# A two-layer hybrid diffusion step on one core: where the three branch output projections keep their operands, and what they wait for

## The chip, the cores and the metric

One core of a Trainium2 chip runs the whole program. The metric is the time of one execution in device microseconds (us); lower is better. TensorE (PE in the profile) multiplies, VectorE (DVE), ScalarE (ACT) and GpSimd (POOL) work element by element, SyncE (SP) issues all transfers, in the order in which they are written.

## The reference, cut to what matters

Each of two layers takes 1152 tokens (1024 latent, 128 context) of width 1024:

```
h = RMSNorm(x) * (1 + scale) + shift
P = h @ W_in                      # queries, keys, values, z paths, merge gates of all mixers
oa, ob, oc = attention, retention, gated DeltaNet (4 heads of 128 each)
y_b = (rms_norm(o_b) * silu(z_b)) @ W_branch[b]            # b = 0, 1, 2: 512 -> 1024
x = x + gate * ((sum_b sigmoid(G_b) * y_b) @ W_out)
```

In the kernel all tokens stand in the free dimension: h is held as 8 blocks of 128 features by 1152 tokens, every head's output o as 128 by 1152.

## The kernel before, in words

**Precision.** A product in full precision is made of three products of a rounded type: an operand is split into a high part (a cast on ScalarE) and a low part (the rest, a subtraction), and high x high, high x low and low x high are added in PSUM. The normalised input is kept so in two fixed tiles, `hH` and `hL` (8 blocks each). Weights are loaded, cast (L648, ACT) and subtracted (L652, POOL) by `load_w`.

**Streams.** A layer is cut into streams (generators): projections for retention (`rp`), DeltaNet (`fk`, `fq`, `fv`), attention values (`av`) and queries and keys (`prep0` to `prep3`), 12 z paths (`z`), 24 merge gates (`g`), for layer 0 also the next layer's conditioning (`ada`). All of these read `hH` and `hL` (matmuls of L677 and L698). Then there are chains that go from engine to engine: retention (`rm`), DeltaNet (`mid`, `pp`, `scan`), and attention, `mix0` to `mix3`, one for each head, one after another behind the last DeltaNet scan. Each chain ends in `put_o`, which transposes the head's output (L1014), multiplies by the z path (L1016) and stores it in DRAM (`osc`, L1017).

**Branches.** `branch` multiplies four heads by `W_branch`. In the order in which they run, the first is that of retention (`br1`), the second that of DeltaNet (`br2`), the third that of attention (in `fin`, ahead of the product with `W_out`, L1936). Each loads the four heads from `osc` (L1854), casts them (L1855, ACT), subtracts (L1856, DVE) and then makes 24 tiles of 128 features by 384 tokens: 12 matmuls (L1879), a multiplication by the gate (L1882, DVE; the gate's tile comes from DRAM, `ssc`), and from the second branch on an addition (L1884, DVE) of the sum so far, which comes from DRAM too (`ysc`). The first two store the sum to `ysc`; the third writes it, split, into `hH` and `hL`. Before the change the split heads take 8 of 25 pages of SBUF.

**What sets the order.** An emitter picks, again and again, the ready stream that stands first: chains first, then the list `BULK`; a stream may start when those it depends on (third argument of `add`) are done and enough pages are free (`NEED`). Then a list scheduler (`Order`) with a priority for each instruction (`LEAD`, `EVAC` shift it) fixes the order on every engine. The engines keep that order on the chip.

Of the kernel before, what the change touches and what calls it, by code (L numbers as in the profile page):

```python
# [33 lines left out]
LAG = 2  # L34
SGN = 3
QO = 'sync'
NP = ()
EVAC = 32000
SC, BK, PV = (2, 3, 4), (5, 6), 7
SLOW, LATE, SLOWD = 0.93, 0, 1.265  # L40
CHAIN = ('pp', 'scan', 'rm', 'mid', 'mix')
BULK = "rp0 z10 fv0 rp1 fk3 fk0 z11 fq1 z13 fk1 fq0 fv1 z12 fq2 g17 z22 z23 fv2 av0 fv3 z20 g13 prep0 g12 g04 g22 g14 fk2 prep3 av1 prep1 g27 z21 z00 g23 g20 gate0 g21 g10 g11 g26 z01 g00 fq3 g15 z02 g03 g16 g01 g25 g02 g07 prep2 br2 z03 g06 g05 ada fin br1 g24".split()
NEED = {'rp': 10, 'rm': 6, 'fk': 6, 'mid': 4, 'fq': 5, 'fv': 6, 'pp': 2, 'scan': 1, 'av': 10, 'prep': 9, 'mix': 5, 'z': 3, 'g': 3, 'gate': 6, 'ada': 6, 'fin': 16, 'br': 14}
LEAD = {'mix': 4000, 'scan': 0, 'mid': 500, 'pp': 0, 'rm': 0, 'fv': 200, 'prep': 4000, 'fq': 0, 'fa': 1000}

K_CS, K_TRI, K_REL, K_ONE, K_LIN, K_ID, K_BLK, K_MH, K_SEL, K_I32, K_END = (
    0, 1024, 1280, 1536, 1664, 1668, 1796, 1800, 1836, 1838, 1870)
# [506 lines left out]
class Build:  # L554
# [181 lines left out]
    def layer(self, l):  # L736
# [1099 lines left out]
    def branch(self, l, br, bi):  # L1836


        nc, ar, ap = self.nc, self.ar, self.ap
        last = bi == 2  # L1840
        self.store(0)
        seq = [ap["w_branch"][l, br, :, fp * 256:fp * 256 + 256] for fp in range(4)]
        held = []

        def weights():

            while seq and len(held) < (FD if held else 1):
                held.append(self.load_w([seq.pop(0)], 4))
            return held.pop(0)

        hl = []
        for h in range(NH):
            o, hb, lb = ar.alloc(T), ar.alloc(T, True), ar.alloc(T, True)
            nc.sync.dma_start(out=o.v(T), in_=self.osc[l][br][h])  # L1854
            nc.scalar.copy(hb.v(T), o.v(T))  # L1855
            nc.vector.tensor_tensor(out=lb.v(T), in0=o.v(T), in1=hb.v(T).bitcast(F32), op=ALU.subtract)  # L1856
            o.free()
            hl.append((hb, lb))
        tr = Ring(ar, 384, 3)
        pr = Ring(ar, 384, 3) if bi else None  # L1860
        yield 0, 8, 5
        for fp in range(4):
            w, wh, wl = weights()
            for fi in range(2):
                f = 2 * fp + fi
                for tb in range(3):
                    c = slice(tb * 384, tb * 384 + 384)
                    t = tr.next().v(384)
                    nc.sync.dma_start(out=t, in_=self.ssc[l][br][f][:, c])
                    y = t  # L1870
                    if bi:
                        y = pr.next().v(384)
                        nc.sync.dma_start(out=y, in_=self.ysc[l][f][:, c])
                    out = self.ps[:, self.bank(1, (0, 1, 2, 3)) if last else self.bulk(), 0:384]
                    i = 0
                    for hb, lb in hl:
                        h = i // 3
                        for ww, a in ((wh, hb), (wh, lb), (wl, hb)):
                            nc.tensor.matmul(out=out, lhsT=ww[:, h, fi * 128:fi * 128 + 128], rhs=a.v(T)[:, c], start=i == 0, stop=i == 11)  # L1879
                            i += 1  # L1880
                    with self.lead(EVAC):
                        nc.vector.scalar_tensor_tensor(out=t, in0=t, scalar=1.0, in1=out, op0=ALU.add, op1=ALU.mult)  # L1882
                    if bi:
# [147 lines left out]
```

## Time and profile before

| | |
|---|---|
| median of 3 runs (lowest, highest) | 3273.01 us (3272.86 to 3279.33) |
| profiled execution | 3282.82 us |
| its span, first to last instruction | 3281.0 us |
| TensorE busy | 3124.0 us, 95% |
| mean granted clock of TensorE | 0.979 of full speed |

The profiled execution is 9.8 us longer than the median of the timed runs; 1.8 us of its time lie outside the span. The busy share of TensorE counts a matmul from issue to its modelled end, so it says when TensorE had nothing to do, not how near it is to its peak.

### The profile page before, as it was taken

How to read it: one execution, taken by the hardware profiler on the slowest of the kernel's cores; microseconds unless marked ns; L12 is line 12 of the kernel's file. 1: busy time of each engine (PE TensorE's matmuls, PEld its weight loads, DVE VectorE, ACT ScalarE, POOL GpSimd, SP SyncE). 2: the span in 40 equal slices, each digit the busy share in tenths (PEclk: the TensorE clock that was granted, in tenths of full speed). 3: DMA queues.
4: the chain of work that ended last, by engine and by line, in shares of the span. 5: the costliest groups of instructions: out<-in, count | busy, mean ns of one | idle time of the engine just before them, and what ended most of it. 6: DMA issues, size and time to landing. Idle time of an engine off the chain costs nothing.

```text
span 3281.0 us, 59199 instructions
## 1 busy us (share of the span) xinstructions
PE 3124.0 (95%) x22411; PEld 2957.9 (90%) x22411; DVE 1887.3 (58%) x4625; ACT 1358.1 (41%) x3982; POOL 1009.9 (31%) x1366
## 2 busy tenths in 40 slices
PE   7999999999999998979999999999999999979799
PEld 6999999999999987878799998999999989969787
DVE  5536566665355558655455365656654657676452
ACT  5324455354354546522233244544443535554120
POOL 3222244343442213113132214443335143221140
PEclk9999999999999999989999999999999999989999
DMA  6122324423121161278322223233232121124771
GB/s 217 57 84 89 93 72 132 121 64 100 51 64 59 42 204 50 93 237 261 120 84 73 83 79 99 81 97 96 68 94 60 42 69 35 54 71 148 243 254 52
DMA packets 328401, 335.73 MB, mean 102 GB/s; under 512 B 58165, under 2 KB 293043, under 8 KB 328115
## 3 DMA queue, kind: packets, MB, share of 16 engines
q1 hardware_dynamic: 328114, 331.95, 32.3%
q8 instruction: 176, 2.88, 0.4%
q14 instruction: 111, 0.90, 0.1%
HBM read 239.43 MB, written 92.44 MB: 101 GB/s over the span
## 4 chain that ended last, share of the span: by engine, by line
PE 81%; DMA 8%; DVE 5%; ACT 3%; issue 2%; POOL 1%; SPq 0%; DVEq 0%; ACTq 0%; POOLq 0%
PE ps L698 34%; PE ps L677 14%; PE ps L1936 6%; PE ps L1879 5%; PE ps L1772 4%; PE ps L1803 4%; PE ps L1794 2%; DMA pg<-ssc 2%; DMA pg<-in_w_in 1%; PE ps L1582 1%; DMA pg<-in_w_ada 1%; DMA pg<-ysc 1%; PE ps L1577 1%; PE ps L1590 1%; PE ps L1574 1%
## 5 line engine op out<-in xcount | busy, mean ns | idle before, releaser
L698 PE MATMUL ps<-hH,pg 128*128 128x384 f32 x4608 | 1274.2, 346 | 11.1 <-ACT pg L648 5.6
L652 POOL TENSOR_TENSOR pg<-pg,pg 128x256 fp32r<-128x256 f32 (+1 forms) x704 | 549.2, 809 | 1212.7 <-ACT pg L648 777.4
L698 PEld LDWEIGHTS ps<-hH,pg 128*128 128x128 f32 x4608 | 835.8, 189 | 19.9 <-ACT pg L648 6.5
L698 PE MATMUL ps<-hL,pg 128*128 128x384 f32 x2304 | 789.7, 343 | 0.0
L677 PE MATMUL ps<-pg,hH 128*128 128x256 f32 (+1 forms) x2880 | 545.6, 287 | 9.0 <-DVE pg L1683 3.8
L677 PEld LDWEIGHTS ps<-pg,hH 128*128 128x128 f32 x2880 | 449.4, 189 | 16.6 <-DVE pg L1683 6.0
L698 PEld LDWEIGHTS ps<-hL,pg 128*128 128x128 f32 x2304 | 435.0, 189 | 1.6
L677 PE MATMUL ps<-pg,hL 128*128 128x256 f32 (+1 forms) x1440 | 407.6, 284 | 0.6 <-DVE hL L942 0.6
L1879 PE MATMUL ps<-pg,pg 128*128 128x384 f32 x1728 | 336.4, 347 | 53.4 <-ACT pg L648 38.8
L1879 PEld LDWEIGHTS ps<-pg,pg 128*128 128x128 f32 x1728 | 309.3, 193 | 60.2 <-ACT pg L648 40.5
L677 PEld LDWEIGHTS ps<-pg,hL 128*128 128x128 f32 x1440 | 271.5, 189 | 2.1 <-DVE hL L942 0.8
L648 ACT CAST pg<-pg 128x1024 fp32r<-128x1024 f32 (+1 forms) x176 | 184.0, 1049 | 183.6 <-DMA pg<-in_w_in 76.3
L627 POOL TENSOR_TENSOR lo<-lo,kc 128x12 f32<-128x12 f32 (+4 forms) x94 | 143.8, 1530 | 363.4 <-DVE lo L1694 88.1
L1335 DVE SCALAR_TENSOR_TENSOR pg<-pg,lo,pg 128x384 f32<-128x384 f32 (+2 forms) x288 | 191.7, 669 | 72.1 <-ACT pg L1333 67.6
L1772 PE MATMUL ps<-pg,pm 128*128 128x384 f32 x768 | 214.3, 371 | 6.7 <-ACT pg L1776 6.4
L1776 ACT ACTIVATE pg<-ps,lo 128x384 f32<-128x384 f32 (+1 forms) x300 | 168.7, 572 | 82.9 <-DVE lo L1774 81.7
L1773 DVE TENSOR_REDUCE lo<-ps 128x1 f32<-128x384 f32 (+1 forms) x300 | 158.9, 543 | 74.2 <-PE ps L1772 72.4
L1936 PE MATMUL ps<-pg,hH 128*128 128x512 f32 x576 | 185.4, 402 | 5.0 <-POOL pg L652 3.8
L968 ACT ACTIVATE pg<-ps 128x384 f32<-128x384 f32 x144 | 70.6, 490 | 199.0 <-PE ps L698 196.8
L1772 PEld LDWEIGHTS ps<-pg,pm 128*128 128x128 f32 x768 | 130.0, 197 | 21.3 <-ACT pg L1776 14.1
L1803 PE MATMUL ps<-pg,pg 128*128 128x128 f32 x1040 | 141.0, 283 | 8.1 <-ACT pg L1799 4.7
L1803 PEld LDWEIGHTS ps<-pg,pg 128*128 128x128 f32 x1040 | 132.9, 197 | 12.2 <-ACT pg L1799 7.0
(300 smaller groups left out, 4908.1 us busy)
## 6 DMA issues: line engine op xcount, KB each, us to landing
pg<-in_w_in SPq DMA_DIRECT2D x112, 512.0 KB
ssc<-pg SPq DMA_DIRECT2D x144, 192.0 KB
pg<-ssc SPq DMA_DIRECT2D x144, 192.0 KB
pg<-in_w_ada SPq DMA_DIRECT2D x48, 512.0 KB
pg<-gsc SPq DMA_DIRECT2D x32, 576.0 KB
ysc<-pg SPq DMA_DIRECT2D x96, 192.0 KB
pg<-ysc SPq DMA_DIRECT2D x96, 192.0 KB
zsc<-pg SPq DMA_DIRECT2D x72, 192.0 KB
```

The source lines that it names most:

```text
L627: self.nc.gpsimd.tensor_tensor(out=out, in0=in_, in1=self.mh[0:in_.shape[0], 0:in_.shape[1]], op=ALU.pow)
L648: nc.scalar.copy(h, r)
L652: (nc.vector if dve else nc.gpsimd).tensor_tensor(out=lo[:, c], in0=r[:, c], in1=h[:, c].bitcast(F32), op=ALU.subtract)
L677: nc.tensor.matmul(out=out, lhsT=a[:, k, t * 128:t * 128 + 128], rhs=x[:, k % 4, :], start=i == 0, stop=i == 23)
L698: nc.tensor.matmul(out=out, lhsT=w[:, k, :], rhs=a[:, k, tb * 384:tb * 384 + 384], start=i == 0, stop=i == 23)
L1335: nc.vector.scalar_tensor_tensor(out=o, in0=x[:, lo + s:hi + s], scalar=wcol(s), in1=o, op0=ALU.mult, op1=ALU.add)
L1772: nc.tensor.matmul(out=self.ps[:, b, 0:w], lhsT=q[:, i, m], rhs=k, start=i == 0, stop=i == 1)
L1773: nc.vector.tensor_reduce(out=s[:, m * 3 + c:m * 3 + c + 1], in_=self.ps[:, b, 0:w], op=ALU.max, axis=AX.X)
L1776: nc.scalar.activation(out=p.v(T)[:, c * w:c * w + w], in_=self.ps[:, bs[c], 0:w], func=AF.Exp, bias=s[:, 6 + m:7 + m], accum_out=s[:, 8 + ...
L1803: nc.tensor.matmul(out=oo, lhsT=x[:, i * 128:i * 128 + 128], rhs=v, start=kt == 0, stop=kt == nkt - 1)
L1879: nc.tensor.matmul(out=out, lhsT=ww[:, h, fi * 128:fi * 128 + 128], rhs=a.v(T)[:, c], start=i == 0, stop=i == 11)
L1936: nc.tensor.matmul(out=out, lhsT=a, rhs=ww[:, f % 2, :], start=j == 0, stop=j == 23)
```

## The change

The split heads of the first two branches go into `hH` and `hL` (blocks 0 to 3 and 4 to 7), which hold the normalised input until the last projection has read them. So `br1` now depends on every gate, every z path, `av1`, `prep3` and `scan3`; `br2` on `br1` alone. `fin` depends on `mix2` and no longer on `mix3`; its branch loads three heads, and waits for `mix3` (the `yield` ahead of the fourth) before it emits the load of the fourth. `NEED` of branches falls from 14 to 8, of `fin` from 16 to 14. The loads, casts and subtractions of heads get a lead of 600. `EVAC`, three entries of `LEAD` and the list `BULK` are replaced. No matmul is added or removed.

```diff
+HL = 600
-EVAC = 32000
+EVAC = 16000
-BULK = "rp0 z10 fv0 rp1 fk3 fk0 ... g06 g05 ada fin br1 g24".split()
+BULK = "rp1 z10 rp0 fk3 fk0 fv0 ... z03 br1 ada g03 g06 g07".split()
-NEED = {..., 'fin': 16, 'br': 14}
+NEED = {..., 'fin': 14, 'br': 8}
-LEAD = {'mix': 4000, ..., 'prep': 4000, 'fq': 0, 'fa': 1000}
+LEAD = {'mix': 8000, ..., 'prep': 0, 'fq': 8000, 'fa': 4000}
...
-        add("br1", self.branch(l, 1, 0), ["rm1"] + [f"g1{f}" for f in range(8)])
-        add("br2", self.branch(l, 2, 1), ["br1", "scan3"] + [f"g2{f}" for f in range(8)])
-        add("fin", self.finish(l), ["br2", "mix3"] + gs + zs + ["gate0"] * (l == 0) + ["ada"] * (not last))
+        add("br1", self.branch(l, 1, 0), ["rm1", "scan3", "av1", "prep3"] + gs + zs)
+        add("br2", self.branch(l, 2, 1), ["br1"])
+        add("fin", self.finish(l), ["br2", "mix2"] + ["gate0"] * (l == 0) + ["ada"] * (not last))
...
-        hl = []
+        hl, own = [], []
         for h in range(NH):
-            o, hb, lb = ar.alloc(T), ar.alloc(T, True), ar.alloc(T, True)
-            nc.sync.dma_start(out=o.v(T), in_=self.osc[l][br][h])
-            nc.scalar.copy(hb.v(T), o.v(T))
-            nc.vector.tensor_tensor(out=lb.v(T), in0=o.v(T), in1=hb.v(T).bitcast(F32), op=ALU.subtract)
-            o.free()
+            if last and h == NH - 1:
+                yield (f"mix{h}.{l}",)
+            with self.lead(HL):
+                o = ar.alloc(T)
+                if last:
+                    own.append((ar.alloc(T, True), ar.alloc(T, True)))
+                    hb, lb = (x.v(T) for x in own[-1])
+                else:
+                    hb, lb = self.hH[:, 4 * bi + h, :], self.hL[:, 4 * bi + h, :]
+                nc.sync.dma_start(out=o.v(T), in_=self.osc[l][br][h])
+                nc.scalar.copy(hb, o.v(T))
+                nc.vector.tensor_tensor(out=lb, in0=o.v(T), in1=hb.bitcast(F32), op=ALU.subtract)
+                o.free()
             hl.append((hb, lb))
```

Lines ahead of `branch` are one higher in the changed kernel (L678 for L677, L1773 for L1772, L1015 for L1014), those in it ten higher (L1889 for L1879, L1892 for L1882, L1894 for L1884).

**First place: TensorE in layer 0, from the end of the projections.** Before, 143 rows of attention and of its transposes stand between the last projection and the first matmul of a branch; these are the last of them (L1794, L1803: `mix2`; L1014: its `put_o`; from L1752 on `mix3`).

```order
L1794 MATMUL ps<-kc,pg_692_10849 128x128
L1803 MATMUL ps<-pm_3_391,pg_672_10737 128x128
L1014 MATMUL ps<-kc,pg_510_7648 128x128 x9
L1752 MATMUL ps<-kc,pm_10_941 128x128 x4
L1772 MATMUL ps<-pm_143_13013,pm_152_13196 128x128 x4
L1772 MATMUL ps<-pg_812_13011,pm_103_9388 128x384 x2
L1752 MATMUL ps<-kc,pm_10_941 128x128 x2
L1772 MATMUL ps<-pg_812_13011,pm_103_9388 128x384 x4
L1752 MATMUL ps<-kc,pm_10_941 128x128 x2
L1794 MATMUL ps<-kc,pg_189_2692 128x128
L1879 MATMUL ps<-pg_801_12388,pg_848_13276 128x384
```

Now the first matmul of the first branch (L1889, on `hH`) stands 18 rows behind the last projection (L678), in the midst of `mix2`.

```order
L678 MATMUL ps<-pg_805_12391,hH 128x256
L678 MATMUL ps<-pg_804_12390,hL 128x256
L1720 MATMUL ps<-kc,pg_742_11982 128x128 x3
L1795 MATMUL ps<-kc,pg_691_10842 128x128 x4
L1773 MATMUL ps<-pg_709_11056,pm_104_9383 128x384 x6
L1804 MATMUL ps<-pg_657_10282,pg_672_10731 128x128 x4
L1795 MATMUL ps<-kc,pg_691_10842 128x128
L1889 MATMUL ps<-hH,pg_801_12382 128x384
L1889 MATMUL ps<-hL,pg_801_12382 128x384
```

What moved: 161 matmuls of the first branch in layer 0 and 220 in layer 1 stand ahead of the `put_o` of `mix2`, where none stood; in layer 1 the first of them is 5 rows behind the last projection.

**Second place: TensorE in layer 0, at the `put_o` of `mix3`.** Before, its transposes stand in the last quarter of the first branch (241 of its 288 matmuls are ahead of them).

```order
L1879 MATMUL ps<-pg_843_13236,pg_865_13694 128x384
L1879 MATMUL ps<-pg_801_12388,pg_849_13277 128x384
L1014 MATMUL ps<-kc,pg_759_12172 128x128 x6
L1879 MATMUL ps<-pg_804_12396,pg_849_13277 128x384
L1879 MATMUL ps<-pg_801_12388,pg_865_13694 128x384
```

Now they stand in the midst of the second (its operands are in `hH` and `hL` too).

```order
L1889 MATMUL ps<-hH,pg_879_13950 128x384
L1889 MATMUL ps<-hL,pg_879_13950 128x384
L1015 MATMUL ps<-kc,pg_759_12166 128x128 x6
L1889 MATMUL ps<-hH,pg_844_13302 128x384
L1889 MATMUL ps<-hH,pg_879_13950 128x384
```

What moved: 425 of the 864 branch matmuls of layer 0 are ahead of these transposes (241 before), and 471 in layer 1 (216 before); 439 and 393 are left behind them.

**Third place: VectorE within `mix3` of layer 0.** Before, between the maxima, sums and copies of attention (L1756 to L1804), a branch needs only the multiplication by the gate (L1882).

```order
L1781 SCALAR_TENSOR_TENSOR lo<-lo 128x1
L1773 TENSOR_REDUCE lo<-ps 128x1
L1882 SCALAR_TENSOR_TENSOR pg_846_13240<-pg_846_13240,ps 128x384
L1783 SCALAR_TENSOR_TENSOR pg_727_11714<-pg_727_11714,lo,pg_189_2692 128x1152
L1774 TENSOR_REDUCE lo<-lo 128x1
L1882 SCALAR_TENSOR_TENSOR pg_846_13240<-pg_846_13240,ps 128x384
L1773 TENSOR_REDUCE lo<-ps 128x1
```

Now the second branch's additions (L1894), whose operand comes from `ysc`, stand there as well.

```order
L1784 SCALAR_TENSOR_TENSOR pg_829_13165<-pg_829_13165,lo,pg_825_13158 128x1152
L1892 SCALAR_TENSOR_TENSOR pg_872_13883<-pg_872_13883,ps 128x384
L1775 TENSOR_REDUCE lo<-lo 128x1
L1757 SCALAR_TENSOR_TENSOR pm_103_9382<-ps,pm_103_9382 128x256
L1894 TENSOR_TENSOR pg_789_12296<-pg_789_12296,pg_872_13883 128x384
L1798 COPY pg_735_11806<-ps 128x512
```

What moved: from the last token of `mix2` to the `put_o` of `mix3` there are now 25 gate products, 11 additions and 4 subtractions of heads in layer 0 (20, none and 2 before), and 23, 14 and 5 in layer 1 (18, none and 2 before).

## Rows read from the trace of the kernel before

**Rows 1.** Page, part 1: busy us, share of the span and instructions of each engine.

```profile
PE 3124.0 (95%) x22411; PEld 2957.9 (90%) x22411; DVE 1887.3 (58%) x4625; ACT 1358.1 (41%) x3982; POOL 1009.9 (31%) x1366
```

**Rows 2.** Two waits of PE, whole span: us, times, longest.

```profile
PE ps L1879 <- ACT pg L648: 38.8, 4, 17.0
PE ps L1879 <- DVE pg L1882: 14.5, 11, 3.4
```

**Rows 3.** Stretches outside layer ends: length, busy us (records) PE PEld DVE ACT POOL, PEclk, DMA share, GB/s.

```profile
82.00:1281.35 1199.35, 1182.82 (x9216) 1136.99 (x9215) 689.78 (x1810) 529.32 (x1626) 408.81 (x561) 1.00 0.28 85
...
1640.00:2874.20 1234.20, 1218.02 (x9075) 1173.59 (x9074) 720.64 (x1831) 546.43 (x1654) 426.97 (x587) 1.00 0.25 74
```

**Rows 4.** Timeline of PE: last projection of each layer.

```profile
1281.06 0.29 PE L677 MATMUL ps<-pg,hL 128*128 128x256 f32 x1
...
2873.89 0.28 PE L677 MATMUL ps<-pg,hL 128*128 128x256 f32 x1
```

**Rows 5.** Four stretches at the end of each layer, columns as in rows 3.

```profile
1281.35:1334.90 53.55, 34.95 (x179) 27.21 (x177) 39.60 (x93) 28.91 (x83) 11.54 (x10) 0.79 0.29 97
1334.90:1431.30 96.40, 94.91 (x616) 91.26 (x615) 65.48 (x156) 46.00 (x150) 17.29 (x21) 0.99 0.45 143
1431.30:1448.30 17.00, 0.00 (x1) 0.01 (x1) 4.63 (x4) 6.51 (x6) 2.09 (x3) 0.63 0.79 286
1448.30:1563.90 115.60, 106.47 (x577) 104.21 (x578) 67.44 (x114) 22.05 (x32) 29.59 (x37) 0.97 0.77 248
2874.20:2941.80 67.60, 47.70 (x237) 38.84 (x235) 48.92 (x117) 35.92 (x109) 10.39 (x10) 0.77 0.21 70
2941.80:3041.70 99.90, 95.88 (x615) 91.91 (x615) 64.32 (x148) 46.70 (x148) 18.09 (x21) 0.98 0.45 146
3041.70:3056.85 15.15, 0.01 (x2) 0.00 (x1) 4.54 (x4) 5.41 (x5) 2.08 (x3) 0.67 0.76 248
3056.85:3170.10 113.25, 106.11 (x577) 103.87 (x578) 66.83 (x112) 21.01 (x30) 30.11 (x37) 0.97 0.79 257
```

**Rows 6.** The same for line L1879 alone: busy us (records) of PE and PEld.

```profile
1334.90:1431.30 96.40, 60.80 (x288) 50.42 (x288) 0.99 0.45 143
...
1448.30:1563.90 115.60, 106.44 (x576) 103.86 (x576) 0.97 0.77 248
```

**Rows 7.** Timeline of PE: 72 branch matmuls without a break.

```profile
1480.13 12.90 PE L1879 MATMUL ps<-pg,pg 128*128 128x384 f32 x72 [0.89 <-DVE pg L1882]
```

**Rows 8.** A stretch within `mix3`, all engines; then L1879 alone.

```profile
1345.00:1405.00 60.00, 59.56 (x410) 57.31 (x409) 44.88 (x109) 34.74 (x114) 2.85 (x4) 1.00 0.37 117
...
1345.00:1405.00 60.00, 29.89 (x137) 23.68 (x137) 1.00 0.37 117
```

**Rows 9.** Timeline of ACT: the second branch's first head, its last weights before matmuls.

```profile
1431.12 1.15 ACT L1855 CAST pg<-pg 128x1152 fp32r<-128x1152 f32 x1 [17.01 <-PE ps L1879]
...
1447.20 1.04 ACT L648 CAST pg<-pg 128x1024 fp32r<-128x1024 f32 x1 [1.29 <-DMA pg<-in_w_branch]
```

**Rows 10.** DVE groups by shape: busy, mean ns, idle before and what ended it.

```profile
L1882 DVE SCALAR_TENSOR_TENSOR pg<-pg,ps 128x384 f32<-128x384 f32 x144 | 78.7, 550 | 86.9 <-DMA pg<-ssc 62.1 <-PE ps L1879 24.2
...
L1884 DVE TENSOR_TENSOR pg<-pg,pg 128x384 f32<-128x384 f32 x96 | 58.4, 620 | 22.5 <-DMA pg<-ysc 21.3
...
L1856 DVE TENSOR_TENSOR pg<-pg,pg 128x1152 fp32r<-128x1152 f32 x24 | 33.5, 1397 | 32.0 <-POOL pg L652 18.6 <-ACT pg L1855 12.4 <-PE ps L1879 0.9
```

**Rows 11.** Chain that ended last: a head's store, two loads of heads (start, us).

```profile
2936.60 4.10 DMA osc<-pg
...
1429.99 7.70 DMA pg<-osc
...
3040.21 4.61 DMA pg<-osc
```

**Rows 12.** The 20 us in which the transfers moved most, columns as in rows 3.

```profile
1500.00:1520.00 20.00, 15.19 (x77) 14.56 (x76) 7.26 (x15) 3.18 (x5) 5.59 (x8) 0.91 0.95 323
```

More of the change, by code (lines that the diff above doesn't have):

```diff
@@ L41 @@
 CHAIN = ('pp', 'scan', 'rm', 'mid', 'mix')
-BULK = "rp0 z10 fv0 rp1 fk3 fk0 z11 fq1 z13 fk1 fq0 fv1 z12 fq2 g17 z22 z23 fv2 av0 fv3 z20 g13 prep0 g12 g04 g22 g14 fk2 prep3 av1 prep1 g27 z21 z00 g23 g20 gate0 g21 g10 g11 g26 z01 g00 fq3 g15 z02 g03 g16 g01 g25 g02 g07 prep2 br2 z03 g06 g05 ada fin br1 g24".split()
-NEED = {'rp': 10, 'rm': 6, 'fk': 6, 'mid': 4, 'fq': 5, 'fv': 6, 'pp': 2, 'scan': 1, 'av': 10, 'prep': 9, 'mix': 5, 'z': 3, 'g': 3, 'gate': 6, 'ada': 6, 'fin': 16, 'br': 14}
-LEAD = {'mix': 4000, 'scan': 0, 'mid': 500, 'pp': 0, 'rm': 0, 'fv': 200, 'prep': 4000, 'fq': 0, 'fa': 1000}
+BULK = "rp1 z10 rp0 fk3 fk0 fv0 fq1 g17 fv3 fq2 fk1 z13 z11 fv2 z20 z22 fv1 z12 z23 g27 fq0 g04 g12 av0 prep0 g13 av1 prep1 g14 g22 fk2 prep3 z21 z00 g23 gate0 g21 g20 z01 g10 g11 g26 g00 fq3 fin g15 z02 g24 g05 prep2 g16 g01 g25 br2 g02 z03 br1 ada g03 g06 g07".split()
+NEED = {'rp': 10, 'rm': 6, 'fk': 6, 'mid': 4, 'fq': 5, 'fv': 6, 'pp': 2, 'scan': 1, 'av': 10, 'prep': 9, 'mix': 5, 'z': 3, 'g': 3, 'gate': 6, 'ada': 6, 'fin': 14, 'br': 8}
+LEAD = {'mix': 8000, 'scan': 0, 'mid': 500, 'pp': 0, 'rm': 0, 'fv': 200, 'prep': 0, 'fq': 8000, 'fa': 4000}
 K_CS, K_TRI, K_REL, K_ONE, K_LIN, K_ID, K_BLK, K_MH, K_SEL, K_I32, K_END = (
@@ L1878, in branch @@
                         for ww, a in ((wh, hb), (wh, lb), (wl, hb)):
-                            nc.tensor.matmul(out=out, lhsT=ww[:, h, fi * 128:fi * 128 + 128], rhs=a.v(T)[:, c], start=i == 0, stop=i == 11)
+                            nc.tensor.matmul(out=out, lhsT=ww[:, h, fi * 128:fi * 128 + 128], rhs=a[:, c], start=i == 0, stop=i == 11)
                             i += 1
@@ L1892, in branch @@
                         self.free_w(w)
-                        for x in hl:
+                        for x in own:
                             self.free_w(x)
```

## The prediction

> **What bounds the kernel now.** The page's first part says that PE is busy 95% of the span [rows 1], so I ask first where the other 5% lies. Cutting the span at the last projection of each layer [rows 4] gives two long stretches in which PE idles 1199.35 − 1182.82 = 16.5 us and 1234.20 − 1218.02 = 16.2 us at a granted clock of 1.00 [rows 3]. The change's moves lie mainly outside them. What stands behind the last projection I cut in four [rows 5]: A, the tail of `mix2`, with nothing to fill it; B, `mix3` with `br1` beside it; C, a hole of 17.00 and 15.15 us in which PE makes no matmul; D, `br2` and the third branch, 576 matmuls [rows 6]. The hole is the longest of the waits on a weight cast [rows 2], but the weights are not its cause: the first head of `br2` is loaded at 1429.99 [rows 11] and cast at 1431.12, once `br1`'s last matmul has let go of pages, and the last cast before a matmul is at 1447.20 [rows 9]. The granted clock falls to 0.79 and 0.77 of the full level (2.4 GHz) in A and to 0.63 and 0.67 in C, after PE had idled there; half of full is the other level, 1.2 GHz [rows 5].
>
> **How much there is to win.** Busy time can't say what PE needs, so I take prices from stretches in which it hardly stops. 72 branch matmuls in a row take 12.90 us, 0.179 each [rows 7]. In 60 us within `mix3` there are 410 records with 0.44 us idle, 137 of them branch matmuls [rows 8]: 137 × 0.179 = 24.5 us, and the other 273 in the remaining 35.1 to 35.5 us, 0.130 each. Length less need, by the counts of [rows 5, 6]:
> - A: layer 0, 53.55 − 179 × 0.13 = 30.3; layer 1, 67.6 − 237 × 0.13 = 36.8.
> - B: 96.4 − (288 × 0.179 + 328 × 0.13) = 96.4 − 94.2 = 2.2; layer 1, 99.9 − 94.1 = 5.8.
> - C: 17.0 and 15.15.
> - D: 115.6 − 103.2 = 12.4; 113.25 − 103.2 = 10.05.
>
> That is 61.9 and 67.8 us, together 129.7. No matmul is added or removed, so this is what layer ends can return at most.
>
> **The change, part by part.** Now br1's heads go where the input was. By the order on PE its first matmul stands 18 rows (layer 0) or 5 rows (layer 1) behind the last projection, and 161 and 220 of its matmuls stand ahead of `put_o` of `mix2`, where A had no filler. `br2` needs no pages for heads and goes on behind `br1`, still within `mix3`. So A's loss and C go, and I price what is left in each layer.
>
> *a) The start of `br1`.* Casts into `hH` must wait for the last projection's reads. They are four of 1.15 us on ACT [rows 9], with subtractions of 1.40 on DVE [rows 10] behind each; their loads can run ahead, since they land in a page. Four of each one after another would be 4.6 + 1.4 = 6 us, of which the mix2 rows between hide one or two. At the low end 1 us (matmuls begin with the first head), at the high end 17, as from first cast to first matmul in [rows 9], if loads and weights come late. I take 5.
>
> *b) Waits inside `mix3`.* Before, 2.2 and 5.8 with br1's gate products as filler. Now VectorE does more between the last token of `mix2` and `put_o` of `mix3`: 5 gate products, 11 additions and 2 subtractions more in layer 0, 5 × 0.55 + 11 × 0.62 + 2 × 1.40 = 12.4 us, and 5, 14 and 3 in layer 1, 15.6 [rows 10]. On 65.5 and 64.3 busy of some 96 to 100 us [rows 5] that makes about 78 and 80: still less than PE's need. The lower bound is no wait, the upper is that of the slower rival below. I take 5.
>
> *c) Lead of 600 for heads.* The casts, subtractions and loads are as many as before, 12 to a layer. ACT, which does the casts, is busy 46 of 96 us in B [rows 5], so I give this 0; without that cover it is a).
>
> *d) The fourth head of the third branch.* It is emitted after `put_o` of `mix3`: multiplication by the z path (taken as a gate product, 0.55 [rows 10]), store 4.10, load 4.61 to 7.70 [rows 11], cast 1.15 [rows 9], subtraction 1.40 [rows 10], together 11.8 to 14.9 us. Meanwhile 146 (layer 0) and 100 (layer 1) matmuls of `br2` are left for PE, 26 and 18 us at 0.179, so PE has cover. But in VectorE's queue the subtraction has only 5 and 4 of `br2`'s gate products ahead; one comes each 12 × 0.179 = 2.15 us, 10.8 and 8.6 us, and two PSUM banks carry PE 4.3 us further: 15.1 and 12.9. That just covers. I take 1 (0 to 2); without cover it would be 12 to 15.
>
> *e) Transfers behind `mix3`.* The 439 and 393 branch matmuls left there need 78.6 and 70.3 us. By the order on SP 23.2 and 21.4 MB of transfers go with them (weights, sums, gates, W_out); before, 35.7 and 37.2 MB went with 623 and 648 matmuls. At the rate of D, 248 and 257 GB/s [rows 5], they take 93.5 and 83.3 us, a loss of 15 and 13. At 323 GB/s, the best 20 us, with a DMA share of 0.95 [rows 12], 72 and 66: no loss. D's loss scaled to the matmuls left gives 9.4 and 6.9. I take 11 and 10.
>
> A rule speaks for more room here: the Trainium skill, "DMA: Bandwidth & Descriptors", section "Bandwidth", gives 425 GB/s measured for 16 MB with one core streaming. By that 23.2 MB would take an estimated 55 us and term e) would be nothing. No stretch here shows such a rate; the best stretch stays at 323.
>
> *f)* Weights at the turn to `br2` and to W_out: a wait of 1.3 us on a transfer stands before such a cast [rows 9]; I take 1.
>
> *g) The other lists.* `EVAC`, `LEAD`, `NEED` and `BULK` reorder a layer's body. At the last `put_o` of DeltaNet 4183 projection matmuls are done in layer 0 where there were 4272, and 4176 for 4260 in layer 1; at that of `mix1` 5400 for 5400 and for 5358. The work is the same and PE idles 16.5 and 16.2 us in a body [rows 3]: I take 0, and ±8, a half of one body's idle time.
>
> The sum left is 5 + 5 + 1 + 11 + 1 = 23 in layer 0 and 22 in layer 1: 45 of 129.7, a gain of 85. The profiled execution took 3282.8 us, so its like would be 3198. The median of timed runs is 9.8 us below that execution, and 3273 − 85 = 3188.
>
> **The rivals.**
> - *Transfers are no bound* (0.08). With `br2` half done before `mix3` ends, its sums and weights are loaded early and e) vanishes: gain 106, 3167 us. For it: 323 GB/s is moved for 20 us [rows 12]. Against: the mean of D is no more than 257 [rows 5]. The page named above would have it so.
> - *The hole comes back ahead of `br1`* (0.10). If casts, loads and weights line up as in [rows 9], a) is 17 instead of 5 in each layer: gain 61, 3212 us. For it: only 5 rows of `mix2` stand between in layer 1. Against: loads needn't wait for `hH`, and br1's weights can be loaded before.
> - *The bodies get worse* (0.08). If attention runs short of filler, or its first pages come late, and the idle of both bodies doubles (33 us), the gain is 52: 3221 us. The place is the last quarter of a body, where fewer projections are left in reserve before and more after.
> - *Nothing moves* (0.04). It needs the loss of A and C, 98 us in all, to turn up again elsewhere, for example in PE waiting for heads in A. A change within 0.2%, 6.5 us, is about what a measurement of this kernel can't tell from none.
> - *Slower, by VectorE's queue* (0.06). In `mix3` 36 gate products and additions in layer 0 (25 and 11) and 37 in layer 1 (23 and 14) read tiles that come from DRAM. DVE runs in order, so maxima and sums of attention are queued behind a late tile, and PE's next scores wait for those. Waits so far are 86.9 / 144 = 0.60 us for each product and 22.5 / 96 = 0.23 for each addition [rows 10], together 17.6 and 17 us, just under the 18 and 20 that DVE has free there. The forecast gives each layer 42 us, so it turns slower if waits exceed 18 + 42 = 60 us a layer, 1.6 us for each of 36 operations. At 2.5 each, 90 − 18 = 72 lost against 42 won in each layer: about 60 us slower, 3333. Against it: the longest waits of PE on such a product were 3.4 us, 11 in all [rows 2], with transfers at a share of 0.77 [rows 5]; in B it is 0.45.
>
> **How the numbers follow.** The forecast has 0.64 and covers gains of about 65 to 112: the bounds of e) (0 to 28), ±8 of g), b) from 2 to 10. The range of 3152 to 3230 takes in the hole, the slipping bodies and transfers that don't bind, with a margin; what is left out is the no-change and slower cases and the ends of a), some 0.15. Faster holds 0.64 + 0.08 + 0.10 + 0.08 = 0.90, the same 0.04, slower 0.06.
>
> **What the profile after would show.** If I am right: records of L1889 between the last projection and `put_o` of `mix2`, the granted clock there at 0.95 or more, and PE idle below 8 us in it; no stretch of 15 us without matmuls before `br2`, and L649's cast no longer the first of PE's waits; PE's waits on L1892 the largest, behind `mix3`, at a DMA share of 0.80 or more; no more than 2 us before the fourth head's matmuls; bodies of 1200 ± 8 and 1234 ± 8 us. I am wrong if DVE's waits on `ssc` and `ysc` within `mix3` grow past 60 us, if the last projection itself moves later by more than 8 us, or if PE stands after it for loads of heads.

## The result, and the profile after

The changed kernel takes 3166.26 us (median of 4 runs, 3162.39 to 3169.71) where the kernel before took 3276.17 beside it (3272.86 to 3280.33): a ratio of 0.9664, 95% interval 0.9643 to 0.9685. That is 109.9 us less. 85 were forecast (3188 us); the range reached from 3152 to 3230. The profiled execution took 3169.7 us with a span of 3167.9, against 3281.0 before, so the two profiles are 113.1 us apart.

The page's first part, which answers to [rows 1]:

```profile
PE 3084.9 (97%) x22411; PEld 2938.7 (93%) x22411; DVE 1886.3 (60%) x4625; ACT 1355.4 (43%) x3982; POOL 1007.7 (32%) x1366
```

The same 22411 matmuls; PE's busy time is 39 us shorter, and the mean granted clock of the execution is 0.991 for 0.979. PE's largest waits, whole span (us, times, longest), which answer to [rows 2]:

```profile
PE ps L1889 <- DVE pg L1892: 11.3, 11, 1.6
...
PE ps L1889 <- ACT pg L649: 4.0, 3, 3.0
```

The wait on a weight cast, 38.8 us with single waits up to 17.0 before, is 4.0, and none is longer than 3.0. Now the whole span, cut at the last projection, the first branch matmul, `put_o` of `mix2`, that of `mix3`, and the last branch matmul of each layer (columns as in [rows 3]; the stretches answer to [rows 5], but C has no counterpart):

```profile
0.00:1278.50 1278.50, 1244.93 (x9837) 1192.62 (x9838) 745.92 (x1946) 578.12 (x1746) 426.57 (x599) 0.99 0.31 96
1278.50:1285.55 7.05, 4.52 (x22) 3.33 (x21) 7.05 (x12) 7.05 (x15) 0.57 (x1) 0.85 0.52 160
1285.55:1334.40 48.85, 44.77 (x272) 41.52 (x271) 34.31 (x69) 20.32 (x48) 23.49 (x25) 0.99 0.70 229
1334.40:1429.40 95.00, 91.83 (x605) 87.08 (x604) 74.89 (x183) 50.48 (x161) 13.09 (x15) 1.00 0.51 162
1429.40:1514.10 84.70, 79.93 (x446) 77.34 (x445) 53.73 (x92) 18.67 (x29) 27.33 (x32) 1.00 0.82 264
1514.10:2812.20 1298.10, 1288.18 (x9426) 1236.26 (x9425) 761.05 (x1916) 573.61 (x1712) 439.32 (x607) 1.00 0.26 79
2812.20:2816.10 3.90, 0.92 (x7) 0.41 (x4) 3.90 (x5) 3.83 (x8) 0.00 (x0) 0.99 0.87 277
2816.10:2887.60 71.50, 66.72 (x396) 63.66 (x397) 47.76 (x101) 28.06 (x73) 23.78 (x24) 0.93 0.57 179
2887.60:2981.80 94.20, 91.11 (x596) 87.44 (x596) 75.74 (x177) 51.48 (x160) 13.30 (x17) 0.98 0.56 176
2981.80:3061.20 79.40, 72.88 (x403) 69.91 (x403) 49.56 (x84) 18.18 (x29) 27.75 (x32) 1.00 0.77 249
3061.20:3167.90 106.70, 99.09 (x419) 79.09 (x417) 32.35 (x45) 5.55 (x7) 12.48 (x16) 0.98 0.26 96
```

And the branch's line alone in the same stretches (PE and PEld):

```profile
1285.55:1334.40 48.85, 35.12 (x174) 30.21 (x175) 0.99 0.70 229
1334.40:1429.40 95.00, 55.16 (x259) 44.31 (x258) 1.00 0.51 162
1429.40:1514.10 84.70, 77.93 (x434) 75.36 (x433) 1.00 0.82 264
...
2816.10:2887.60 71.50, 46.23 (x228) 40.69 (x228) 0.93 0.57 179
2887.60:2981.80 94.20, 53.83 (x250) 43.58 (x250) 0.98 0.56 176
2981.80:3061.20 79.40, 69.81 (x388) 67.06 (x387) 1.00 0.77 249
```

`mix2`'s tail now holds 174 and 228 branch matmuls, where A held none; from the last projection to `put_o` of `mix2` the granted clock is 0.97 and 0.93, where A had 0.79 and 0.77. `br2` starts with no hole. The loss that A had by the unit prices was in part idle time (53.55 − 34.95 = 18.6 us, and 19.9 in layer 1 [rows 5]) and in part matmuls that took longer than their price; no run tells what of the second part was the clock.

For comparison the span before, cut more coarsely: up to the last projection; the end of layer 0 (to its last branch matmul); the body of layer 1 (to its last projection); the end of layer 1; the tail with W_out:

```profile
0.00:1281.35 1281.35, 1242.88 (x9796) 1186.76 (x9797) 736.33 (x1933) 574.19 (x1727) 434.06 (x599) 0.99 0.30 94
1281.35:1563.90 282.55, 236.32 (x1370) 222.69 (x1369) 177.16 (x367) 103.47 (x269) 60.50 (x71) 0.92 0.57 186
1563.90:2874.20 1310.30, 1291.93 (x9390) 1232.39 (x9390) 757.20 (x1900) 564.76 (x1688) 442.77 (x609) 0.99 0.25 77
2874.20:3170.10 295.90, 249.70 (x1429) 234.62 (x1428) 184.62 (x380) 109.04 (x290) 60.68 (x71) 0.91 0.54 176
3170.10:3281.00 110.90, 103.11 (x433) 81.41 (x431) 32.02 (x49) 6.62 (x9) 11.93 (x16) 0.98 0.27 93
```

Where the 113.1 us come from: the ends of the layers are 47.0 (282.55 to 235.6) and 46.9 us shorter (295.9 to 249.0), the first stretch 2.9, the body of layer 1 12.2, the tail 4.2. With the unit prices of the prediction (0.179 and 0.130 us) the loss in the ends (length less what their matmuls need at these prices) falls from 129.0 to 42.6 us, by 86.4; the other 7.4 us of the ends' shortening are some 60 matmuls fewer to make in them, which now run in the bodies.

### The profile page after: what moved, and what is told of

The parts are those of the page before. It is cut to its first block, busy times and chain, and to the rows that moved or that the text cites. A ratio compares the mean times of both kernels' runs of the same rounds, so it can differ in the third digit from the quotient of the medians.

```text
span 3167.9 us, 59152 instructions
## 1 busy us (share of the span) xinstructions
PE 3084.9 (97%) x22411; PEld 2938.7 (93%) x22411; DVE 1886.3 (60%) x4625; ACT 1355.4 (43%) x3982; POOL 1007.7 (32%) x1366
## 4 chain that ended last, share of the span: by engine, by line
PE 61%; DMA 7%; DVE 3%; issue 2%; ACT 1%; POOL 0%; SPq 0%; DVEq 0%; POOLq 0%; ACTq 0%
PE ps L699 22%; PE ps L678 12%; PE ps L1946 6%; PE ps L1773 4%; PE ps L1889 4%; PE ps L1804 4%; DMA pg<-ssc 2%; PE ps L1795 2%; DMA pg<-ysc 1%; DMA pg<-in_w_in 1%; DMA ysc<-pg 1%; DMA pg<-in_w_branch 1%; PE ps L1583 1%; PE ps L1578 1%; PE ps L1591 1%
## 5 line engine op out<-in xcount | busy, mean ns | idle before, releaser
L699 PE MATMUL ps<-hH,pg 128*128 128x384 f32 x4608 | 1265.6, 345 | 2.4 <-DVE pg L1656 0.9
L699 PEld LDWEIGHTS ps<-hH,pg 128*128 128x128 f32 x4608 | 835.0, 188 | 9.8 <-DVE pg L1656 1.1
L678 PE MATMUL ps<-pg,hH 128*128 128x256 f32 (+1 forms) x2880 | 550.9, 287 | 3.3 <-ACT hH L942 2.0
L678 PEld LDWEIGHTS ps<-pg,hH 128*128 128x128 f32 x2880 | 454.3, 190 | 5.8 <-ACT hH L942 2.6
L678 PE MATMUL ps<-pg,hL 128*128 128x256 f32 (+1 forms) x1440 | 412.5, 288 | 1.1 <-DVE hL L943 1.1
L678 PEld LDWEIGHTS ps<-pg,hL 128*128 128x128 f32 x1440 | 272.4, 190 | 3.1 <-DVE hL L943 1.5
L1889 PE MATMUL ps<-hH,pg 128*128 128x384 f32 x768 | 213.3, 346 | 6.5 <-DVE pg L1892 3.2
L1773 PE MATMUL ps<-pg,pm 128*128 128x384 f32 x768 | 216.6, 366 | 1.9 <-ACT pg L1777 1.5
L1889 PEld LDWEIGHTS ps<-hH,pg 128*128 128x128 f32 x768 | 140.3, 190 | 9.4 <-DVE pg L1892 4.4
L1804 PE MATMUL ps<-pg,pg 128*128 128x128 f32 x1040 | 138.3, 281 | 5.2 <-ACT pg L1800 5.2
L1804 PEld LDWEIGHTS ps<-pg,pg 128*128 128x128 f32 x1040 | 130.7, 195 | 8.6 <-ACT pg L1800 6.7
L1773 PEld LDWEIGHTS ps<-pg,pm 128*128 128x128 f32 x768 | 125.3, 192 | 12.4 <-ACT pg L1777 4.5
```

The lines of the kernel that those rows point to most:

```text
L678: nc.tensor.matmul(out=out, lhsT=a[:, k, t * 128:t * 128 + 128], rhs=x[:, k % 4, :], start=i == 0, stop=i == 23)
L699: nc.tensor.matmul(out=out, lhsT=w[:, k, :], rhs=a[:, k, tb * 384:tb * 384 + 384], start=i == 0, stop=i == 23)
L1773: nc.tensor.matmul(out=self.ps[:, b, 0:w], lhsT=q[:, i, m], rhs=k, start=i == 0, stop=i == 1)
L1804: nc.tensor.matmul(out=oo, lhsT=x[:, i * 128:i * 128 + 128], rhs=v, start=kt == 0, stop=kt == nkt - 1)
```

## The experiments

Each ratio is to the kernel before, run beside it. To compare runs with each other, I put each ratio on one time of before, 3276 us.

| run | median us | before beside it | ratio (95%) | gain at 3276 |
|---|---|---|---|---|
| changed kernel | 3166.26 | 3276.17 | 0.9664 (0.9643 to 0.9685) | 110 |
| e1_lists_only | 3274.41 | 3279.09 | 0.9987 (0.9977 to 0.9997) | 4 |
| e2_place_only | 3208.83 | 3279.09 | 0.9790 (0.9775 to 0.9805) | 69 |
| e3_fin_waits | 3168.78 | 3279.09 | 0.9666 (0.9648 to 0.9684) | 109 |
| e4_br1_pages | 3246.28 | 3279.09 | 0.9903 (0.9889 to 0.9918) | 32 |
| e6_old_bulk | 3179.32 | 3279.19 | 0.9694 (0.9660 to 0.9727) | 100 |
| e7_old_lead | 3216.26 | 3279.19 | 0.9803 (0.9775 to 0.9831) | 65 |
| e11_br1_after_mix2 | 3220.80 | 3281.06 | 0.9813 (0.9792 to 0.9833) | 61 |
| e12_prep_lead | 3181.65 | 3281.06 | 0.9697 (0.9672 to 0.9722) | 99 |
| e13_heads_no_lead | 3171.00 | 3281.06 | 0.9662 (0.9645 to 0.9680) | 111 |

### Lists alone, place alone

`e1_lists_only`, from the kernel before:

```diff
-EVAC = 32000
+EVAC = 16000
-BULK = <before>
+BULK = <after>
-LEAD = {'mix': 4000, ..., 'prep': 4000, 'fq': 0, 'fa': 1000}
+LEAD = {'mix': 8000, ..., 'prep': 0, 'fq': 8000, 'fa': 4000}
```

> The kernel before with the new EVAC, BULK and LEAD alone; heads stay in pages and the branches wait for what they waited for. My theory (the gain comes from the operands' new place, the lists bring nothing of their own): 3276 within 10 us; no branch matmul stands beside mix2 and the hole of 15 to 17 us before the second branch is still there in each layer. Rival (the lists bring most of the 110 us): below 3220. In between: by the order on PE 83 and 122 rows of mix2 are left behind the last projection where there were 115 and 160, so by the loss of about 0.17 us for each such row in stretch A some 12 us could come back: 3264.

Measured: 4 us of gain. Stretches A of this run and the body between them:

```profile
1277.80:1333.50 55.70, 32.58 (x137) 25.01 (x135) 34.26 (x77) 24.21 (x66) 11.31 (x10) 0.66 0.28 91
...
1561.60:2863.80 1302.20, 1290.35 (x9437) 1236.30 (x9436) 763.65 (x1922) 572.20 (x1713) 439.62 (x608) 1.00 0.26 77
2863.80:2931.70 67.90, 40.77 (x192) 32.68 (x190) 41.83 (x95) 29.36 (x83) 11.75 (x11) 0.71 0.23 76
```

In each A 42 and 45 fewer matmuls are left than in [rows 5] (137 for 179, 192 for 237), yet A lasts as long as before: 55.7 and 67.9 us for 53.55 and 67.6. So the expectation of 12 us by rows was wrong: A is not the sum of its rows, it is a chain of attention with a length of its own, and work taken out of it only makes it emptier.

`e2_place_only`, from the changed kernel:

```diff
-HL = 600
+HL = 0
-EVAC, BULK, LEAD = <after>
+EVAC, BULK, LEAD = <before>
```

> The changed kernel with the EVAC, BULK and LEAD of before and no lead for heads: place of operands, dependencies and three heads alone. My theory: 85 us of the gain stay, 3191 within 10. Rival (place and lists only work together): by the order on PE 93 and 117 matmuls of the first branch stand ahead of put_o of mix2 where the changed kernel has 161 and 220; if the 171 that are missing cost their 0.179 us each in later stretches, 30 us are lost: 3197 to 3225. If the place brings little: above 3250.

Measured: 69 us of gain, 3208.8 us, in the midst of the second case. The place alone brings 69, the lists alone 4, both together 110: some 37 us belong to neither alone. With the place alone `mix2`'s tail holds 98 and 125 branch matmuls, and 485 and 472 are left behind `mix3`.

### Which list

`e6_old_bulk` and `e7_old_lead` put one list of before into the changed kernel, `e12_prep_lead` one entry of it (`'prep': 4000`), `e13_heads_no_lead` takes the heads' lead away (`HL = 0`).

> The changed kernel with the list BULK of before. By the order on PE 457 and 461 branch matmuls stand ahead of put_o of mix3 (425 and 471 in the changed kernel). Theory L (of the lists LEAD alone decides how much branch work stands ahead of mix3's end): no loss, 3160 to 3170. Rival B (BULK gives the bodies of the layers their gain of some 15 us): 3175 to 3185.

> The changed kernel with the LEAD of before. By the order on PE 373 and 385 branch matmuls stand ahead of put_o of mix3, 52 and 86 fewer than in the changed kernel. Theory L: each of these costs 0.18 to 0.25 us behind mix3, 25 to 34 us in all: 3191 to 3200. Rival B: 3170 or less. Rival E (EVAC and the lead of heads matter as much): halfway, 3175 to 3188.

> The changed kernel with one entry of LEAD as before: prep 4000 where the change has 0. By the order on PE 417 and 441 branch matmuls stand ahead of put_o of mix3 (425 and 471), 38 fewer. If what counts is how many stand there: 8 to 10 us lost, 3174 to 3176. Rival (this entry is most of what the old LEAD cost, 50 us, whatever stands there): 3195 or more. Rival (no effect): 3163 to 3169.

> The changed kernel without the lead of 600 for the loads, casts and subtractions of heads. My prediction took this lead as 0 us: 3163 to 3169. By the order on PE 416 and 441 branch matmuls stand ahead of put_o of mix3 (425 and 471); if these count, 8 to 10 us are lost: 3174 to 3176.

Measured: without the new `LEAD` 45 us are lost, more than the 25 to 34 expected; without the new `BULK` 10; by the one entry 11; without the heads' lead none (expected by the prediction; by the count of matmuls it would have been 8 to 10). The intervals of the runs that lose 10 and 11 overlap that of the changed kernel, so these sizes are uncertain. `e6_old_bulk` lies in the case in which `BULK` counts: its last projection of layer 0 comes at 1284.2 for 1278.5, its ends are 4.5 us longer, the body of layer 1 only 1.4. `e12_prep_lead` lies between the first case and the second. `EVAC` and `NEED` had no run of their own. `e7_old_lead`, from `mix2`'s tail to the end of the branches in both layers:

```profile
1296.30:1340.70 44.40, 37.01 (x212) 32.07 (x212) 33.94 (x67) 22.21 (x55) 25.44 (x24) 0.88 0.50 162
1340.70:1437.70 97.00, 95.88 (x629) 92.28 (x629) 75.19 (x180) 48.79 (x159) 14.81 (x15) 1.00 0.51 162
1437.70:1537.60 99.90, 90.88 (x487) 87.54 (x487) 58.25 (x100) 20.86 (x31) 27.42 (x32) 0.97 0.81 257
...
2843.90:2914.00 70.10, 58.38 (x347) 52.51 (x347) 52.15 (x109) 33.50 (x96) 22.14 (x22) 0.93 0.43 139
...
3007.20:3109.90 102.70, 92.44 (x486) 88.60 (x485) 59.64 (x100) 21.31 (x32) 28.05 (x32) 0.95 0.80 256
```

From the last projection (1286.3 and 2838.8) on, the tail of `mix2` lasts as long as in the changed kernel (54.4 and 75.2 us for 55.9 and 75.4), but holds 96 and 145 branch matmuls for 174 and 228; what is missing stands in `mix3` and behind it (486 and 474 behind, for 434 and 388), and by the unit prices the loss of both ends is 70.0 us for 42.6. The other 18 us: the last projection of layer 0 is 7.8 us later (1286.3 for 1278.5), some 11 us are 80 more matmuls left to make in the ends, the body of layer 1 is 3 us longer, and the tail with W_out 3 shorter.

### Is it the work beside mix2?

`e11_br1_after_mix2`, from the changed kernel:

```diff
-add("br1", self.branch(l, 1, 0), ["rm1", "scan3", "av1", "prep3"] + gs + zs)
+add("br1", self.branch(l, 1, 0), ["rm1", "mix2", "av1", "prep3"] + gs + zs)
```

> The changed kernel, but the first branch waits for mix2 where it waited for the last DeltaNet scan; its heads still lie in hH and hL. By the order on PE 50 and 66 matmuls of it stand ahead of put_o of mix2 (161 and 220 in the changed kernel), 301 and 304 ahead of that of mix3 (425 and 471). Theory A (the gain is branch work that runs beside mix2, where PE would stand): the 111 and 154 matmuls that leave mix2 cost at least their 0.179 us each, 47 us, and up to 73 if the 291 that then stand behind mix3 cost 0.25 each: 3213 to 3239. Rival P (the gain is the pages that come free and the hole that goes): 3175 or less.

Measured: 49 us lost, 3220.8, within the range of theory A. Heads still lie in `hH` and `hL`, pages are as free as in the changed kernel. The stretch up to the first branch matmul and that up to `put_o` of `mix2`, in each layer:

```profile
1275.60:1310.40 34.80, 15.96 (x59) 11.33 (x58) 25.07 (x47) 18.37 (x39) 6.92 (x5) 0.57 0.52 176
1310.40:1335.30 24.90, 19.95 (x116) 18.73 (x115) 11.74 (x23) 7.98 (x22) 11.96 (x13) 0.85 0.29 93
...
2840.80:2869.80 29.00, 10.00 (x42) 7.42 (x39) 24.61 (x53) 17.02 (x34) 9.83 (x7) 0.65 0.58 199
2869.80:2908.70 38.90, 33.49 (x203) 29.94 (x204) 21.16 (x43) 15.25 (x45) 11.54 (x12) 0.91 0.28 88
```

PE idles 18.8 and 19.0 us in the first of these, and the clock is at 0.57 and 0.65 again: A's loss is back. By the unit prices these stretches lose 66.7 us in both layers, the changed kernel's two (7.05 and 48.85 us, 3.9 and 71.5) 20.9: 45.8 us more. (Behind `mix3` 10 more are lost, within it 8 fewer.) So 49 of the 110 us are shown to come from work beside `mix2`'s tail, and this run still has 55 and 71 branch matmuls there. The other 61 us (the hole, the branch work still there, the bodies) are divided further only in part, by the runs above and below.

`e4_br1_pages`, from the changed kernel: the first branch as before, only the second in `hH` and `hL`.

```diff
-                if last:
+                if last or bi == 0:
                     own.append((ar.alloc(T, True), ar.alloc(T, True)))
...
-add("br1", ..., ["rm1", "scan3", "av1", "prep3"] + gs + zs)
-add("br2", ..., ["br1"])
+add("br1", ..., ["rm1"] + [f"g1{f}" for f in range(8)])
+add("br2", ..., ["br1", "scan3", "av1", "prep3"] + gs + zs)
```

> The changed kernel with the first branch's heads in pages and its old dependencies (and 14 pages needed); only the second branch's heads lie in hH and hL. By the order on PE no branch matmul stands beside mix2. My theory: the loss of stretch A comes back (30 and 37 us, or 55 in all with the fewer rows of mix2 that are left), the hole does not: 3221 to 3233. Rival (it is the pages: the hole comes back, because the second branch is held up by something else than its heads' pages): 3250 or more. Rival (the gain was the hole alone): 3175 or less.

Measured: 3246.3, a gain of 32 us: 78 are lost, between the cases. A loses 36.3 and 42.6 us by the unit prices, 58 more than the changed kernel there; behind `mix3` 24.2 and 21.0 are lost, 32 more. The hole is smaller, and not gone:

```profile
1416.70:1552.50 135.80, 118.50 (x624) 115.33 (x624) 74.77 (x123) 25.18 (x35) 40.38 (x48) 0.94 0.82 257
...
3005.20:3138.90 133.70, 116.56 (x632) 111.09 (x631) 75.54 (x124) 25.78 (x36) 40.75 (x48) 0.97 0.83 267
1416.70:1435.70 19.00, 10.29 (x47) 9.31 (x46) 7.98 (x9) 4.27 (x4) 3.96 (x4) 0.88 0.97 319
...
3005.20:3024.00 18.80, 8.93 (x49) 7.97 (x47) 8.42 (x9) 4.12 (x4) 3.92 (x4) 0.94 0.99 337
```

In the first 19 us behind `mix3` PE idles 8.7 and 9.9 us, at a DMA share of 0.97 and 0.99. Its longest wait, at the end of this stretch, 5.64 us in layer 0 and 7.67 in layer 1, is for the cast of `br2`'s weights. The chain of work before that cast, in layer 0 (start, us):

```profile
1424.11 4.47 PE ps L1889 x16
1428.59 6.02 DMA pg<-in_w_branch
...
1434.68 1.05 ACT pg L649
...
1435.78 0.69 PE ps L1889
```

The weights' load (0.5 MB) is issued only when a matmul of `br1` has ended that still used a page, and then takes 6.02 us, 8.03 in layer 1, among transfers that fill the engines. So what is left of the hole waits for a page again, now for weights, and then for a slow load; taking the heads out of the pages returns only a part of it. In the changed kernel `br2` starts in the midst of `mix3`, and those transfers with it.

This run also shows what filling `mix2`'s tail is worth, since its tail has the rows of attention of the changed kernel, 118 and 173, and no branch matmul. From the last projection to `put_o` of `mix2`:

```profile
1276.50:1324.20 47.70, 26.25 (x118) 19.71 (x116) 28.44 (x61) 20.44 (x54) 11.33 (x10) 0.73 0.25 83
2852.70:2913.80 61.10, 34.91 (x173) 28.61 (x172) 35.67 (x80) 25.33 (x71) 11.90 (x12) 0.74 0.20 66
```

The changed kernel takes 55.9 and 75.4 us there, 8.2 and 14.3 more, and makes 174 and 228 branch matmuls in it, which need 31.1 and 40.8 us at 0.179. So 49 of these 72 us are won, not all: the filler also makes the chain longer.

### Do transfers bind behind mix3?

`e9_no_sum` (from the changed kernel) and `e10_pages_no_sum` (from the run above) leave out the third branch's loads of the sum:

```diff
-nc.sync.dma_start(out=y, in_=self.ysc[l][f][:, c])
+if last:
+    y = t
+else:
+    nc.sync.dma_start(out=y, in_=self.ysc[l][f][:, c])
```

> The changed kernel, but the third branch loads no sum of the other two and adds its own gate product to itself instead, so the sum of the first two branches is left out of the result; 24 loads of 0.197 MB, 4.7 MB, are gone in each layer. Theory D (transfers still bind behind mix3): 18 us of transfers are gone in each layer, more than the loss of 5.5 and 8.0 us there, and 8 to 12 us of it come back: 3154 to 3160. Rival (the loss is VectorE's or that of weights): 3163 to 3168.

> As the run with the first branch's heads in pages (3246 us), and the third branch loads no sum, so that the first two branches are left out of the result. Behind the end of mix3 that run loses 24 and 21 us at 257 and 267 GB/s. Theory D (with the hole gone, transfers bind): 4.7 MB less in each layer are 18 us less each, 32 to 37 in all: 3209 to 3216. Rival (PE waits for the order of weights, heads or VectorE there): 8 us or less: 3238 or more.

Measured: 3161.65 and 3252.82 us, one run each. The second is 6.5 us above the median of the run with pages, where 32 to 37 were to come back: there theory D is refuted in the form in which I put it, and the time lies in its rival's case (3238 or more). The first is 4.6 us below the changed kernel's median, between its two cases; set against the kernel before beside it (3279.19) as in the table, it would be at 3158.6, within theory D's range. So its time alone does not decide, but its stretch behind `mix3` does, here in both layers:

```profile
1425.00:1513.80 88.80, 83.20 (x450) 80.80 (x449) 53.33 (x92) 19.01 (x30) 27.36 (x32) 0.96 0.66 208
2981.10:3055.40 74.30, 72.39 (x401) 69.20 (x400) 50.35 (x85) 18.16 (x29) 28.03 (x32) 1.00 0.69 220
```

and of the second run, in layer 0 and layer 1, its first 19 us and what is left:

```profile
1418.00:1437.00 19.00, 9.16 (x49) 8.20 (x48) 8.11 (x9) 4.40 (x4) 3.10 (x5) 0.93 1.02 334
1437.00:1553.00 116.00, 106.35 (x578) 103.89 (x578) 68.25 (x115) 21.14 (x32) 36.80 (x44) 0.95 0.69 214
...
3009.50:3029.00 19.50, 9.15 (x49) 8.18 (x48) 8.31 (x9) 4.71 (x5) 4.17 (x5) 0.89 1.00 338
3029.00:3147.00 118.00, 109.92 (x589) 104.55 (x590) 66.29 (x114) 21.22 (x32) 34.27 (x44) 0.97 0.68 213
```

In the first run the DMA share falls from 0.82 and 0.77 to 0.66 and 0.69, and the loss there is 9.0 and 3.2 us for 5.5 and 8.0, 12.2 in all for 13.5: the mean rate of the whole stretch is not what binds. In the second run some 10 us of the loss lie in each of the first stretches, which come ahead of the loads that were left out and show a full share; there transfers, with the late weights of the section before, can hold PE up for a short time. The other 13 us of each layer's loss come at a share of 0.69 and 0.68, where transfers do not fill the engines. What ends the smaller waits of the changed kernel is not settled by these runs; the trace names the DVE's waits on tiles that come from DRAM (14.4 us on `ysc`, 13.3 on `ssc` behind `mix3` of layer 0), and SP's own waits until DVE has let go of such tiles (11.8 and 10.7 us), so late issue through three buffers would fit. Another number of buffers was not tried.

### The fourth head

`e3_fin_waits`, from the changed kernel:

```diff
-add("fin", self.finish(l), ["br2", "mix2"] + ...)
+add("fin", self.finish(l), ["br2", "mix3"] + ...)
```

> The changed kernel, but the last stage depends on mix3, so that all four heads are loaded behind it. My theory: the path is 12 to 15 us for the first head and 1.2 to 1.4 for each of the others, 15 to 20 us, against a cover of 15 and 13 us: 2 to 7 us lost in each layer, 3170 to 3180. Rival (heads and weights line up as in the hole of before): 12 us or more lost in each layer, 3190 or more. Rival (second branch covers it all): 3166.

Measured: no loss (0.9666). But this run did not do what I meant: casts of heads from the end of `mix3` of layer 0 on are, on ACT,

```profile
L1865 ACT CAST pg<-pg x1: 1156/1156/1156, 1439.3 to 1439.3; 128x1152 fp32r<-128x1152 f32 x1
```

one, the fourth. The dependence holds back only where the stream is written; the list scheduler lifts the first three heads to where their data allow, and the order on PE has the same counts as in the changed kernel. So the stream's wait for `mix2` alone, as an edit, is worth nothing that can be measured, and what four heads behind `mix3` would cost stays untried.

### The kernel before once more

> The kernel before, unchanged, for a second profile: the body of layer 1 (last branch matmul of layer 0 to last projection of layer 1) took 1310.3 us in the first, 1298.1 in the changed kernel. If the 12 us belong to the change: 1308 or more again. If the first profile was a slow execution: 1303 or less.

Measured: 3270.79 us, a span of 3269.0.

```profile
0.00:1277.70 1277.70, 1240.70 (x9796) 1184.96 (x9797) 734.97 (x1933) 574.29 (x1727) 434.50 (x599) 0.99 0.31 94
1277.70:1559.10 281.40, 237.58 (x1371) 224.02 (x1370) 178.34 (x369) 103.44 (x269) 61.24 (x71) 0.92 0.58 187
1559.10:2866.20 1307.10, 1287.86 (x9390) 1230.00 (x9389) 759.22 (x1898) 565.01 (x1687) 443.39 (x609) 1.00 0.26 77
2866.20:3159.80 293.60, 247.50 (x1430) 231.72 (x1429) 185.74 (x384) 110.39 (x292) 61.41 (x71) 0.92 0.56 178
3159.80:3269.00 109.20, 101.51 (x432) 80.29 (x430) 30.04 (x46) 5.63 (x7) 11.99 (x16) 1.00 0.27 93
```

The body of layer 1 takes 1307.1 us, between the two cases. Against this profile the change brings 90.4 us in the ends (575.0 to 484.6), 9.0 in the body of layer 1, 2.5 in the tail, and loses 0.8 ahead of the first end: 101.1. So of the 19.3 us outside the ends some 9 may be no more than the difference of two executions, and some 11 are left.

## Why the prediction was right, step by step

The direction, the place and the main mechanism were right: PE's losses stood behind the last projection, the branch's operands in `hH` and `hL` let its matmuls run there, and the run in which `br1` waits for `mix2` gives 49 us back. The sum for the ends, 45 us left of 129.7, was measured as 42.6 of 129.0, but that it came so near is in part luck: term a) was 10.9 us too small in both layers together, b) and d) to f) were 13.3 too large. Its terms, in layer 0 and layer 1:

- *a) start of `br1`*: 5 and 5 forecast. Until its first matmul 4.2 and 2.9 are lost; PE waits 2.98 us for a weight cast in layer 1. But the rest of `mix2`'s tail loses 5.0 and 8.8 more, for which the sum had no term: together 9.2 and 11.7. This term was too small.
- *b) waits inside `mix3`*: 5 forecast, 3.7 and 4.5 measured. VectorE is busy 74.9 and 75.7 us there, 78 and 80 were forecast. The slower rival does not show: its waits on `ssc` and `ysc` in these stretches add up to 2.1 and 0.5 us in the rows of its largest waits, 60 would have been needed.
- *c) lead of heads*: 0 forecast; no difference in `e13_heads_no_lead`.
- *d) fourth head*: 1 forecast. In layer 0 `put_o` of `mix3` ends at 1429.4, the cast starts at 1442.2, the subtraction at 1443.4 and takes 1.35: a path of 15.4 us, half a microsecond above the forecast's end of 14.9. PE's waits in the time are 0.76 and 0.18 us, both for the third branch's weights. The cover held.
- *e) and f) behind `mix3`*: 12 and 11 forecast, 5.5 and 8.0 measured. The rates are 264 and 249 GB/s, as in D; but the 84.7 and 79.4 us hold some 22.4 and 19.8 MB (rate by length), less than the 23.2 and 21.4 counted, and the run without the sum shows that bytes over the whole stretch are not what sets its length. Here the rival that transfers are no bound was nearer than the forecast, and its 3167 is nearest to the measured time, but by luck: it got there with a) too small and g) at nothing.
- *g) the other lists*: 0 with ±8 forecast. This is the term that made the forecast too high: outside the ends 19.3 us by the one profile of before, 10.7 by the other, both beyond the ±8, and 7.4 in the ends from some 60 matmuls that moved into the bodies. The forecast saw the moved rows in the order (4183 projections for 4272) and took them as worth nothing, since before they were: A did not get shorter by having less in it, as `e1_lists_only` shows. Once branch work fills A, what is taken out of it counts: of the 45 us that the old `LEAD` costs, 27 are losses in the ends and some 11 are matmuls left in them.

The page that the prediction weighed, the Trainium skill, "DMA: Bandwidth & Descriptors", section "Bandwidth", gives 425 GB/s for one large streaming load. In the runs here a share of 0.97 to 1.02 of the DMA engines goes with 319 to 338 GB/s, so for this mix of loads and stores the measured figure decides.

Right as well: no wait of PE on a weight cast is above 3.0 us, PE idles 6.6 and 7.8 us between the last projection and `put_o` of `mix2` (below 8 forecast). The clock of 0.95 or more there was right in layer 0 (0.97, with 0.85 in the first 7 us) and wrong in layer 1 (0.93). Wrong too: the DMA share of 0.80 behind `mix3` in layer 1 (0.77), and the body of layer 1, 12.2 us shorter where at most 8 was forecast.

What stays open: why the body of layer 1 is shorter with any part of the change (1302.2 us with the lists alone at 9437 matmuls, 1302.8 with the place alone at 9387, before 1307.1 and 1310.3 at 9390), what ends the waits that are left behind `mix3`, and the single entries of `LEAD`, `EVAC` and `NEED`.

## What to carry to other kernels

A stretch in which one chain runs alone has a length of its own: moving rows out of it gained nothing here, and putting other work beside it gained most of that work's time, 49 of 72 us; the chain got longer by the rest. So two edits can be worth 69 and 4 us alone and 110 together, and what a list of priorities is worth has to be priced again once a change has made its stretch the place where work counts. A tile that is dead after its last reader is a place for operands that need no pages; ask then which stretch the work can move to, and what it asks of the queues when it starts there.

## What had not been expected of the hardware

Two executions of the kernel before, profiled, took 3282.8 and 3270.8 us, and differ a little in every stretch: 3.7 us up to the first end, 1.2, 3.2, 2.3 and 1.7 in the others. A difference of 3 or 4 us between stretches of two single profiles, or of 12 between their spans, can so be no more than that of two executions. With 24 loads fewer in each layer the DMA share behind `mix3` fell by 0.16 and 0.08, and the two stretches together took 163.1 us for 164.1.
